# Output projection of a two-layer mixer trunk: four of eight column blocks as two seven-product pairs

## The chip, the cores and the metric

One core of a Trainium2 chip runs the whole program. The metric is device time in microseconds of one execution, the median over runs. Engines: TensorE (PE) multiplies, VectorE (DVE), ScalarE (ACT) and GpSimd (POOL) work on elements, SyncE (SP) issues the DMAs.

## The reference, cut to what matters

Two layers of width 1024 over 1024 tokens, and a final norm. The change lies in the last lines of each layer: three branch outputs are projected, gated and summed, the sum goes through one 1024 x 1024 output projection, is scaled per channel and added to the residual.

```python
def hybrid_layer(x, ...):
    ...
    proj = h @ w_in
    ...
    y = jnp.einsum('btnw,nwd->btnd', branches, w_branch)
    gates = jax.nn.sigmoid(gate_logits.reshape(B, T, N_BRANCHES, D))
    merged = jnp.sum(gates * y, axis=2)
    return x + gate * (merged @ w_out)

def reference(...):
    for l in range(DEPTH):
        x = hybrid_layer(x, ...)
    return rms_norm(x, final_g)
```

## The kernel before, in words

**Layout.** Everything is held transposed: channels on the 128 partitions, tokens along the row. The tokens form two halves `h` of 512 (HF), the 1024 channels eight blocks `d` of 128. An output tile (d, h) is one PSUM accumulator of 128 x 512; there are three of them (`acc_ps`, pool `psa`).

**Split operands.** Each fp32 operand is split into a high part `hi` (a copy rounded to fp32r, made on ScalarE) and a low part `lo` = x - hi (made on GpSimd or VectorE); function `split`. A product is three matmuls, hi x hi, hi x lo and lo x hi (`mm1`, `mm3`), so a block of 128 x 512 weights (four k-tiles of 128) takes 12 matmuls, and a column of the output projection over a token half (eight k-tiles) 24.

**Order.** Nothing is issued while the code runs. Each call is recorded as an `Op` in a `Log`; `Log.plan` then simulates the engines with costs of its own and gives every engine a fixed order, smallest key first among what is ready (the key is about the place in the program). All is issued from one line, 548, so every row of the profile reads L548, and rows are told apart by tiles. `plan` also has buffers handed out in order of first use, keeps GpSimd and VectorE instructions with several SBUF inputs apart in its own time, and may move a GpSimd `tensor_tensor` of the plain lanes to VectorE (`flex`); an instruction written for VectorE stays there. Side work (norms, splits of branch outputs, adaLN columns) runs as generators in lanes ("norm", "norm2", "ada", ...), advanced by `pump` between matmuls; `finish` forces one to its end.

**Weights.** `plan_layer` yields the items of a layer in order; `wprep` loads the next item (two 256 KB tiles `wr`, 128 x 512 each) and splits it into `wh`, `wl` (three buffers each), ahead of use (`wready`). The input projection ends with pairs of items computed as seven block products in place of eight (item "forms"; `wforms` makes the weight forms, `form` the operand forms, `prod` issues one product of 12 matmuls).

**Branches and merge.** Items ("br", n, d) for n = 0, 1, 2 and d = 0, 2, 4, 6 project branch n to blocks d and d + 1. Each tile is scaled by its gate (VectorE, PSUM input) and added into `m`, a slice of four 128 x 2048 tiles `mt` (tag r8, four buffers in all). After branch 2 each (d, h) is split into `mhi`, `mlo` (`merged[d][h]`).

**Output projection.** Part 0 takes half 0 for d = 0 to 7, part 1 half 1. In the second layer half 1 is done in two parts of 256 tokens, and the weights of columns 2 to 7, split in part 0, are kept for parts 1 and 2. Each column: load the residual tile `xres`, 24 matmuls, then on VectorE xres = acc * mod + xres, then the sum of squares (`sq_acc`: square on ScalarE, add on VectorE). In the first layer each result is stored to `xd` and, at the end of a half, `norm_task` makes the next layer's operands of that half (`hhi`, `hlo`) in lane "norm2"; the second layer starts with three items of half 0, then of half 1, whose weights (`wbig`) are loaded at the end of part 1. In the second layer `final_task` norms and stores each part.

Of the kernel before, what the change touches and what calls it, by code (L numbers as in the profile page):

```python
# [9 lines left out]
F32 = mybir.dt.float32  # L10
# [10 lines left out]
L = 2  # L21
# [49 lines left out]
def BR(n, *ds):  # L71
    return [("br", n, d) for d in ds]
# [489 lines left out]
def trunk_kernel(ctx, tc, xT, cvec, pos, vecs, consts, w_ada, w_all, pool_w, lora_w, out):  # L562
# [26 lines left out]
    def nm(s):  # L589
        uid[0] += 1  # L590
        return f"{s}_{uid[0]}"
# [384 lines left out]
    def plan_layer(l):  # L976
        yield from [("lora",)] + RW(0)
        pools = deque(PL(i) for i in range(4))
        gates = deque(GT(0, *range(8)) + GT(1, *range(8)) + GT(2, *range(8)))
        done = 0  # L980
        while done < 4 or prog.get((l, 3), 0) < 10 or pools:
            if done < 4 and prog.get((l, done), -1) >= 0:
                done += 1
                if done < 4:
                    yield from RW(done)
                if l == 0 and done == 1:
                    yield from pools.popleft()
# [12 lines left out]
        rest = list(gates) + [("wg", i) for i in range(4)]  # L1000
        yield ("forms", [(rest[i], rest[i + 1]) for i in range(0, len(rest), 2)])
        for n in range(3):
            yield from BR(n, 0, 2, 4, 6)
# [5 lines left out]
    wready = deque()  # L1009

    def wprep(big=False):
        if wready and wready[-1][0][0] == "forms":
            return
        for l, it in planner:
            if it[0] not in ("merge", "idle", "forms"):
# [7 lines left out]
        if it[0] == "out" and it[1] >= 2 and kept(l):  # L1023
            if it[2]:
                wready.append((it, keep_w[it[1]]))
                return
            if it[1] < 6:
                t = r8("wout")
            else:
                if it[1] == 6:  # L1030
                    keep_w["G"] = gtile("wG")
                t = keep_w["G"][:, 2048 * (it[1] - 6) : 2048 * (it[1] - 5)]
        elif big:
            t = r8("wbig")
        parts = []
        for j in range(2):
# [12 lines left out]
        wready.append((it, parts))  # L1049
# [901 lines left out]
    for l in range(L):  # L1951
# [245 lines left out]
            gates[key] = gs_used[key]("gs")  # L2197
            return gates[key]

        brs = deque((n, d) for n in range(3) for d in (0, 2, 4, 6))  # L2200

        def prefetch():
            for j in range(min(2, len(brs))):
                n, d0 = brs[j]
                for d in (d0, d0 + 1):
                    if (n, d, 0) not in gates:
                        if j and len(gs_free) < 7:
                            return
                        for h in range(2):
                            nc.sync.dma_start(out=gate_tile((n, d, h)), in_=gd[n, d, h])  # L2210

        unsplit = deque()
        next_o(1, 0)
        mt = [r8("mrg") for _ in range(4)]
        merged = [[None, None] for _ in range(8)]
        while wready[0][0][0] != "out":
            it, ws = wready.popleft()
            prefetch()
# [9 lines left out]
            else:  # L2228
                n, d0 = it[1], it[2]
                assert brs.popleft() == (n, d0)  # L2230
                if (n, d0) == (1, 4):
                    next_o(2, 0)
                for d, h in [(d, h) for h in range(2) for d in (d0, d0 + 1)]:
# [5 lines left out]
                    o = (d % 2) * T + h * HF  # L2239
                    m = mt[d // 2][:, o : o + HF]  # L2240
# [7 lines left out]
                    merged[d][h] = m  # L2248
# [10 lines left out]
            finish("ada", task)  # L2259
        h_next = [[], []]  # L2260
        ntask = [None, None]
        if l + 1 < L:
            parts = [(0, slice(0, HF)), (1, slice(0, HF))]
        else:
            parts = [(0, slice(0, HF)), (1, slice(0, HF // 2)), (1, slice(HF // 2, HF))]
        for part, (h, sl) in enumerate(parts):
            if sl.start == 0:
                xs = [None] * 8
                acc = t_rk("ssum")
            for i, d in enumerate(out_order(l, part)):  # L2270
                it, ws = wready.popleft()
                assert it == ("out", d, part)
                last = (i, h) == (7, 1)
# [7 lines left out]
                if sl.start == 0:  # L2281
                    xr = (mi if h == 0 else t_ri if d < 7 else t_rk)("xres")
                    src = xT if l == 0 else xd[0]
                    nc.sync.dma_start(out=xr, in_=src[d, h])
                    xs[d] = xr
                xr = xs[d][:, sl]
# [4 lines left out]
                nc.vector.scalar_tensor_tensor(  # L2291
                    xr, ps, mod[l][:, 16 + d : 17 + d], xr, op0=ALU.mult, op1=ALU.add
                )
                if l + 1 < L:
                    store(xd[0][d, h], xr)
                if d == 7:
                    sq = mo("sq")[:, sl]
                    nc.vector.tensor_tensor(sq, xr, xr, op=ALU.mult)
                    if l + 1 == L:
                        warm = sp.tile([P, 4], F32, tag="rn", name=nm("warm"))[:, 0:1]  # L2300
                        nc.scalar.activation(warm, acc[:, 0:1], AF.Sqrt)
                else:
                    sq_acc(acc[:, sl], xr, i == 0)
                if l + 1 == L:
                    nc.scalar.activation(xr, xr, AF.Copy, scale=vv(0, "final_g", d))
            if l + 1 < L:
                drain("ada")
                ntask[h] = add("norm2", norm_task(l + 1, xs, [acc, sq], h_next[h], 2500 + 2500 * h, h))
            else:
                add("norm", final_task(list(xs), [acc[:, sl], sq], h, sl))  # L2310
# [111 lines left out]
```

## Time and profile before

| | |
|---|---|
| median of 3 runs | 2262.69 us (2262.41 to 2262.93) |
| profiled execution | 2262.4 us; its span, first to last instruction, 2260.6 us |
| granted TensorE clock | 0.997 |
| PE / PEld busy | 2229.0 / 1865.3 us |
| DVE / ACT / POOL busy | 1589.5 / 931.5 / 627.0 us |
| output projection, first layer | about 1060 to 1153 us of the span |
| output projection, second layer | about 2153 to 2251 us |

Times in rows are from the start of the span. A row of a timeline is start, length, engine, line, operation, out<-in, shape, count, and in brackets the idle time of the engine before it with what ended it. A row of groups is engine, operation, tiles, shape, count, then busy time and mean length in ns, then idle time before. A matmul's recorded length (about 0.39 us for 512 columns) overlaps the next one's; the spacing of starts is what it occupies. PEld are the weight loads, which run beside the matmuls.

### The profile page before, as it was taken

To read this page: it belongs to the slowest core of one execution; us is meant where nothing else is said; L and a number is where in the kernel's file an instruction comes from. 1 tells how busy PE (TensorE), PEld (TensorE's weight loads), DVE (VectorE), ACT (ScalarE), POOL (GpSimd) and SP (SyncE) were. 2 spreads that over 40 slices of the span, in tenths; PEclk is the share of its full clock that TensorE was granted. 3 is DMA by queue.
4 is the path that set the end of the run, shared out by engine and by line. 5 is a ranking of instruction groups with operands and counts; after the bars stand their busy time and mean duration, and the time that the engine had idled before them with its cause. 6 is when DMAs were issued, how large, how long until landed. Compare 5 with 4: busy or idle time off the path is not lost.

```text
span 2260.6 us, 34881 instructions
## 1 busy us (share of the span) xinstructions
PE 2229.0 (99%) x12980; PEld 1865.3 (83%) x12980; DVE 1589.5 (70%) x2750; ACT 931.5 (41%) x1795; POOL 627.0 (28%) x564
## 2 busy tenths in 40 slices
PE   7999999999999999999999999999999999999998
PEld 6788888888888888888878888888888888888888
DVE  7996877958878765668667678587686744465854
ACT  5634434434344344323454343353443444442243
POOL 2223323323325233332122132333332500041311
PEclk9999999999999999999999999999999999999999
DMA  8222111112236664654541111111122533256442
GB/s 318 70 59 72 34 43 42 51 46 70 86 119 218 200 201 130 229 187 167 172 134 31 45 41 44 55 38 49 40 82 93 182 112 112 89 184 218 135 131 85
DMA packets 138906, 249.36 MB, mean 110 GB/s; under 512 B 15728, under 2 KB 20080, under 8 KB 138736
## 3 DMA queue, kind: packets, MB, share of 16 engines
q1 hardware_dynamic: 138736, 247.14, 34.1%
q8 instruction: 102, 1.67, 0.3%
q14 instruction: 68, 0.56, 0.1%
HBM read 187.57 MB, written 59.51 MB: 109 GB/s over the span
## 4 chain that ended last, share of the span: by engine, by line
PE 89%; DVE 7%; ACT 2%; issue 1%; DMA 1%; SPq 0%; DVEq 0%; ACTq 0%
PE acc L548 73%; PE two L548 3%; PE ch L548 2%; PE ro L548 1%; PE g L548 1%; PE av L548 1%; DVE two L548 1%; DVE tm L548 1%; DVE ksq L548 1%; PE rs L548 1%; DVE G L548 1%; PE rkv L548 1%; PE m L548 1%; PE bt L548 1%; PE lw L548 1%
## 5 line engine op out<-in xcount | busy, mean ns | idle before, releaser
L548 PE MATMUL acc<-hhi,wh 128*128 128x512 f32 x1488 | 597.1, 401 | 1.6 <-DVE vp L548 1.1
L548 PE MATMUL acc<-hhi,wl 128*128 128x512 f32 x1488 | 596.9, 401 | 0.0
L548 PE MATMUL acc<-hlo,wh 128*128 128x512 f32 x1488 | 596.3, 401 | 0.0
L548 POOL TENSOR_TENSOR wl<-wr,wh 128x512 fp32r<-128x512 f32 x171 | 228.4, 1335 | 585.8 <-ACT wh L548 440.5
L548 PEld LDWEIGHTS acc<-hhi,wh 128*128 128x128 f32 x1488 | 280.5, 189 | 50.8 <-DVE vp L548 1.5
L548 PEld LDWEIGHTS acc<-hhi,wl 128*128 128x128 f32 x1488 | 280.6, 189 | 48.7
L548 PEld LDWEIGHTS acc<-hlo,wh 128*128 128x128 f32 x1488 | 280.6, 189 | 47.3
L548 ACT CAST wh<-wr 128x512 fp32r<-128x512 f32 x242 | 149.3, 617 | 268.3 <-PE acc L548 215.5
L548 PE MATMUL acc<-T,wh 128*128 128x512 f32 x576 | 177.6, 389 | 0.0
L548 PEld LDWEIGHTS acc<-T,wh 128*128 128x128 f32 x576 | 108.1, 188 | 22.4
L548 DVE SCALAR_TENSOR_TENSOR S<-ch,pc,SP 64x64 f32<-64x64 f32 x224 | 63.3, 283 | 87.1 <-PE ch L548 84.3
L548 PE MATMUL acc<-T,wl 128*128 128x512 f32 x288 | 112.1, 389 | 0.0
L548 DVE TENSOR_TENSOR wl<-wsum,wh 128x512 fp32r<-128x512 f32 x63 | 45.3, 719 | 78.7 <-ACT wh L548 78.4
L548 ACT CAST wh<-wsum 128x512 fp32r<-128x512 f32 x96 | 59.5, 620 | 96.6 <-PE acc L548 92.9
L548 ACT COPY Z<-ch 64x128 f32<-64x128 f32 x128 | 33.0, 258 | 132.6 <-PE ch L548 132.0
L548 POOL TENSOR_TENSOR oz<-ol,oz 128x512 fp32r<-128x512 f32 x10 | 14.0, 1401 | 264.8 <-DVE wl L548 179.7
L548 DVE TENSOR_TENSOR tm<-MT,two 64x30 f32<-64x30 f32 (+14 forms) x240 | 76.3, 318 | 11.4 <-ACT two L548 4.6
L548 DVE TENSOR_TENSOR two<-two,tm 64x30 f32<-64x30 f32 (+14 forms) x240 | 78.9, 329 | 7.1
L548 PE MATMUL acc<-oy,wh 128*128 128x512 f32 x256 | 80.1, 394 | 0.0
L548 PE MATMUL acc<-oG,wh 128*128 128x512 f32 x256 | 79.0, 390 | 0.0
L548 PE MATMUL acc<-oz,wh 128*128 128x512 f32 x256 | 78.9, 389 | 0.0
L548 DVE TENSOR_TENSOR wl<-wraw,wh 128x512 fp32r<-128x512 f32 x48 | 33.7, 703 | 63.5 <-ACT wh L548 63.5
(332 smaller groups left out, 4863.5 us busy)
## 6 DMA issues: line engine op xcount, KB each, us to landing
wr<-in_w_all SPq DMA_DIRECT2D x268, 256.0 KB, 2.7
wraw<-in_w_all SPq DMA_DIRECT2D x96, 256.0 KB, 2.7
gd<-gsg SPq DMA_DIRECT2D x96, 256.0 KB, 2.0
gs<-gd SPq DMA_DIRECT2D x96, 256.0 KB, 3.8
wada<-in_w_ada SPq DMA_DIRECT2D x80, 256.0 KB, 2.9
ol<-od SPq DMA_DIRECT2D x48, 256.0 KB, 3.5
traw<-hd SPq DMA_DIRECT2D x32, 256.0 KB, 3.0
x<-in_xT SPq DMA_DIRECT2D x16, 256.0 KB, 5.2
```

Of the source, the lines that this page charges most:

```text
L548: o.inst = f(*a, **k)
```

## The change

Columns d = 0 to 3 leave the column-by-column scheme. Part 0 keeps columns 4 to 7 of half 0. Then a new item ("outs",) computes the pairs (0, 1) and (2, 3) for both halves, each as seven block products: with A the two columns' weights in four blocks (column x k-half) and B the merged operand in four blocks (k-half x token half), products of sums and differences of blocks replace the eighth. Then part 1 (and 2) does columns 4 to 7 of half 1.

- `out_forms(f)`, four tasks in lane "norm2", makes the operand forms: in place on the raw merged tiles (`raw_m`, whose layout in `mt` is changed to one tile per d-half and token half), three subtractions per k for f = 0, one for f = 1, none for 2 and 3; each form is then split, high half on ScalarE, low half on VectorE. Task 0 is added at the last item of branch 2, tasks 1 to 3 at columns 0, 1, 3 of part 0 (`TAT`). Low halves of forms 1 to 3 take an r8 buffer each, high halves of forms 2 and 3 the big tile G.
- `out_pairs` makes the weight forms: four loads, four combinations on VectorE and seven splits with the low half on VectorE (`osplit_w`) per pair.
- Products accumulate in three accumulators; `add_out` adds an accumulator into the residual tile more than once (seven adds in the first pair, six in the second, against four for the same tiles before).
- `wprep`'s low halves of branch 2 and of part 0 are made on VectorE. Branch 2 takes its items in the order 0, 4, 2, 6. In the second layer columns 5 to 7 are kept from part 1 for part 2, column 4 is loaded again.

```diff
+TAT = (0, 1, 3)
+DORDER = ((0, 2, 4, 6), (0, 2, 4, 6), (0, 4, 2, 6))
...
     def out_order(l, part):
-        return (2, 3, 0, 4, 5, 1, 6, 7) if kept(l) and part else range(8)
+        return (5, 6, 4, 7) if part == 2 else (4, 5, 6, 7)
...
         for part in range(2 + (l + 1 == L)):
+            if part == 1:
+                yield ("outs",)
             yield from [("out", d, part) for d in out_order(l, part)]
...
-            split(raw, hi, lo)
+            split(raw, hi, lo, nc.vector if it[0] == "out" and it[2] == 0 or it[:2] == ("br", 2) else nc.gpsimd)
...
+        def out_forms(f):
+            if f == 2:
+                out_G.append(gtile("oT"))
+            if f:
+                oL = r8("oL")
+                los = [oL[:, k * HF : (k + 1) * HF] for k in range(4)]
+            else:
+                los = [t_ri("oL") for _ in range(4)]
...
+            for k in range(4):
+                while any(type(merged[q][h]) is not tuple for q in (k, k + 4) for h in range(2)):
+                    yield 2000
+                b11, b12, b21, b22 = raw_m[k][0], raw_m[k][1], raw_m[k + 4][0], raw_m[k + 4][1]
+                if f == 0:
+                    sub_(b11, b12, b11)
+                    sub_(b12, b22, b12)
+                    sub_(b22, b22, b11)
+                elif f == 1:
+                    sub_(b21, b21, b22)
+                x = (b11, b22, b12, b21)[f]
...
+                nc.scalar.copy(hi, x)
+                nc.vector.tensor_tensor(lo, x, hi.bitcast(F32), op=ALU.subtract)
...
+                for d in (0, 2):
+                    xr = [[residual(d + i, h_) for h_ in range(2)] for i in range(2)]
+                    ca = acc_ps()
+                    prod(ca, lows[0], True)
+                    cd, cb = acc_ps(), acc_ps()
+                    nc.scalar.copy(cb, ca)
+                    if d == 0:
+                        prod(cd, highs[1], True)
+                        add_out(d, xr[0][1], cd)
+                        finish("norm2", otasks[0])
+                        cd = acc_ps()
+                        prod(cd, OT[0], True)
+                        add_out(d + 1, xr[1][1], cd)
+                        add_out(d, xr[0][1], cd)
+                        finish("norm2", otasks[1])
+                        prod(cb, OT[1], False)
+                        add_out(d, xr[0][1], cb)
+                        out_done(d, 1, full, True, False)
+                        prod(ca, highs[0], False)
+                        add_out(d, xr[0][0], ca)
+                        out_done(d, 0, full, False, False)
+                        finish("norm2", otasks[2])
+                    else:
+                        prod(cd, OT[0], True)
+                        add_out(d + 1, xr[1][1], cd)
+                        prod(cb, OT[1], False)
+                        add_out(d, xr[0][1], cb)
+                        prod(ca, highs[0], False)
+                        add_out(d, xr[0][0], ca)
+                        out_done(d, 0, full, False, False)
+                    prod(cb, OT[2], False)
+                    add_out(d + 1, xr[1][1], cb)
+                    out_done(d + 1, 1, full, False, False)
+                    if d:
+                        prod(cd, highs[1], False)
+                        add_out(d, xr[0][1], cd)
+                        out_done(d, 1, full, False, False)
+                    finish("norm2", otasks[3])
+                    prod(cb, OT[3], False)
+                    add_out(d + 1, xr[1][0], cb)
+                    out_done(d + 1, 0, full, False, d == 2)
+                half_done(0, full)
...
+                if part == 0 and i == 3:
+                    source = out_pairs()
+                    ready_w.extend(next(source) for _ in range(2))
+                if part == 0 and i in TAT:
+                    otasks.append(add("norm2", out_forms(len(otasks))))
```

`out_done` is what followed the add before (store, square, final scale); `half_done(0)` starts the norm of half 0 and now stands after the pairs; `residual` loads a residual tile once per (d, h).

More of the change, by code (lines that the diff above doesn't have):

```diff
@@ L2261, in trunk_kernel, with residual @@
         ntask = [None, None]
+        xs = [[None] * 8, [None] * 8]
+        late = deque()
+        acc = [None, None]
+        sqs = [None, None]
+        def residual(d, h):
+            if acc[h] is None:
+                acc[h] = t_vp("ssum")
+            if xs[h][d] is None:
+                if h and d == 2:
+                    late.extend([r8("xres")] * 4)
+                if h and 2 <= d < 6:
+                    xr = late.popleft()[:, (d - 2) * HF : (d - 1) * HF]
+                else:
+                    xr = (mi if h == 0 else t_ri if d < 7 else t_rk)("xres")
+                nc.sync.dma_start(out=xr, in_=(xT if l == 0 else xd[0])[d, h])
+                xs[h][d] = xr
+            return xs[h][d]
@@ new lines, in add_out, with out_done @@
+        def add_out(d, xr, ps):
+            nc.vector.scalar_tensor_tensor(xr, ps, mod[l][:, 16 + d : 17 + d], xr, op0=ALU.mult, op1=ALU.add)
+        def out_done(d, h, sl, first, last):
+            xr = xs[h][d][:, sl]
+            if l + 1 < L:
+                store(xd[0][d, h], xr)
+            if last:
+                sqs[h] = mo("sq")[:, sl]
+                nc.vector.tensor_tensor(sqs[h], xr, xr, op=ALU.mult)
+                if l + 1 == L:
+                    warm = sp.tile([P, 4], F32, tag="rn", name=nm("warm"))[:, 0:1]
+                    nc.scalar.activation(warm, acc[h][:, 0:1], AF.Sqrt)
+            else:
+                sq_acc(acc[h][:, sl], xr, first)
+            if l + 1 == L:
+                nc.scalar.activation(xr, xr, AF.Copy, scale=vv(0, "final_g", d))
@@ new lines, in half_done, with osplit_w @@
+        def half_done(h, sl):
+            if l + 1 < L:
+                drain("ada")
+                ntask[h] = add("norm2", norm_task(l + 1, xs[h], [acc[h], sqs[h]], h_next[h], 2500 + 2500 * h, h))
+            else:
+                add("norm", final_task(list(xs[h]), [acc[h][:, sl], sqs[h]], h, sl))
+        def osplit_w(x):
+            hi = wp.tile([P, HF], F32R, tag="wh", name=nm("wh"), bufs=3)
+            lo = wp.tile([P, HF], F32R, tag="wl", name=nm("wl"), bufs=3)
+            split(x, hi, lo, nc.vector)
+            return hi, lo
@@ new lines, in out_pairs, with loads, comb, forms @@
+        def out_pairs():
+            def loads(d):
+                r = []
+                for it, j in ((("out", d), 0), (("out", d + 1), 0), (("out", d + 1), 1), (("out", d), 1)):
+                    r.append(t_rk("wraw"))
+                    nc.sync.dma_start(out=r[-1], in_=w_all[l, ITEMS.index(it), j])
+                return r
+            def comb(x, y, op):
+                t = t_cs("wsum")
+                nc.vector.tensor_tensor(t, x, y, op=op)
+                return t
+            def forms():
+                for d in (0, 2):
+                    a11, a21, a22, a12 = loads(d)
+                    yield osplit_w(a11)
+                    s1 = comb(a21, a22, ALU.add)
+                    if d:
+                        yield osplit_w(s1)
+                    s2 = comb(s1, a11, ALU.subtract)
+                    if d:
+                        yield osplit_w(s2)
+                    else:
+                        yield osplit_w(comb(a12, s2, ALU.subtract))
+                    if d == 0:
+                        yield osplit_w(s1)
+                        yield osplit_w(s2)
+                    yield osplit_w(a12)
+                    yield osplit_w(comb(a11, a21, ALU.subtract))
+                    if d:
+                        yield osplit_w(comb(a12, s2, ALU.subtract))
+                    yield osplit_w(a22)
+            return forms()
@@ L2280, in trunk_kernel @@
                             wprep()
[L2281 to L2286, printed above, removed]
+                xr = residual(d, h)[:, sl]
                 ps = acc_ps()[:, 0 : xr.free_size()]
@@ L2290, in trunk_kernel @@
                     mm3(ps, ws[j], rhs, j == 0, j == 1)
[L2291 to L2310, printed above, removed]
+                add_out(d, xr, ps)
+                out_done(d, h, sl, part == 0 and i == 0, h == 1 and i == 3)
+            if h == 1:
+                half_done(1, sl)
         drain("norm", "st") if l + 1 == L else None
```

54 lines of the change are left out of this document (38 added, 16 removed).

## The prediction

> **What bounds the kernel now.** I read the page's first and fourth parts first, then the chain of waits in order of time for the long stretches without a break, then a table of busy times over the stages around the output projection, and last VectorE's and GpSimd's timelines there.
>
> ```profile
> span 2260.6 us, 34881 instructions
> PE 2229.0 (99%) x12980; PEld 1865.3 (83%) x12980; DVE 1589.5 (70%) x2750; ACT 931.5 (41%) x1795; POOL 627.0 (28%) x564
> PE 89%; DVE 7%; ACT 2%; issue 1%; DMA 1%; SPq 0%; DVEq 0%; ACTq 0%
> ...
> 1786.80 411.03 PE acc L548 x1807
> 2205.94 19.55 PE acc L548 x163
> 2229.82 20.03 PE acc L548 x167
> ```
>
> TensorE is the bound: 99% busy, 89% of the chain. A busy share says little by itself, since matmuls overlap in the records, so the price of a matmul is its spacing in an unbroken piece of the chain. 1807 matmuls in 411.03 us are 0.2275 us each; that piece runs from the second layer's seven-product pairs of the input projection through the branch products into the output projection, so such pairs already stream without a gap. In the last stretch the matmuls have 256 columns: 163 in 19.55 and 167 in 20.03 us, 0.1199 us each. Two of them do one wide matmul's work in 0.2398 us.
>
> The stages, from the last branch's product (n = 2) of the first layer through its two output halves to the start of the second layer, and the second layer's last branch product and output halves. Columns after the window: its length, then busy time and count by engine, clock, DMA share, GB/s.
>
> ```profile
> 1016.50:1060.20 43.70, 43.70 (x192) 35.78 (x191) 37.61 (x47) 13.31 (x22) 11.31 (x9) 1.00 0.51 171
> 1060.20:1104.00 43.80, 43.80 (x199) 36.38 (x198) 23.42 (x34) 15.43 (x25) 1.39 (x2) 1.00 0.47 148
> 1104.00:1148.00 44.00, 44.00 (x203) 36.69 (x202) 31.51 (x43) 22.59 (x37) 14.81 (x12) 1.00 0.59 193
> 1148.00:1180.00 32.00, 30.20 (x144) 24.67 (x143) 24.77 (x38) 20.03 (x36) 10.04 (x12) 1.00 0.45 143
> ...
> 2109.00:2153.00 44.00, 44.00 (x192) 35.82 (x191) 38.52 (x47) 12.85 (x22) 13.23 (x10) 1.00 0.43 136
> 2166.00:2210.00 44.00, 44.00 (x237) 38.09 (x236) 19.89 (x31) 18.11 (x31) 5.16 (x4) 1.00 0.35 106
> ```
>
> In every stage that the change touches TensorE has no idle time except 1.8 us at the start of the second layer. So fewer matmuls shorten the run, unless what they need comes later. VectorE is next: 86% in the branch stage (37.61 of 43.70), 53% in the first output half.
>
> **The matmuls removed.** A column of 128 outputs over half of the tokens takes 8 x 3 = 24 matmuls. First layer now: 8 columns x 2 halves x 24 = 384 wide ones, 87.4 us. After: part 0 has 4 x 24 = 96, the two pairs 2 x 7 x 12 = 168, part 1 another 96, together 360, 81.9 us: 5.5 us less. Second layer now: 192 wide and 384 narrow ones, 192 x 0.2275 + 384 x 0.1199 = 89.7 us. After: 96 + 168 wide and 192 narrow, 60.1 + 23.0 = 83.1 us: 6.6 us less, since the pairs also run at full width what ran in halves. Together **12.1 us**, with 24 + 120 = 144 matmuls fewer.
>
> **VectorE's load, the cover of everything else.** What a VectorE instruction costs there:
>
> ```profile
> 1011.23 0.69 DVE L548 SCALAR_TENSOR_TENSOR gs<-gs,acc 128x512 f32<-128x512 f32 x1 [1.36 <-PE acc L548]
> 1011.84 0.69 DVE L548 TENSOR_TENSOR oG<-ol,oG 128x512 fp32r<-128x512 f32 x1
> 1012.44 1.79 DVE L548 TENSOR_TENSOR mrg<-mrg,gs 128x512 f32<-128x512 f32 x1
> ...
> 1058.44 1.29 POOL L548 TENSOR_TENSOR wl<-wr,wh 128x512 fp32r<-128x512 f32 x1 [6.02 <-ACT wh L548]
> 1058.53 1.75 DVE L548 TENSOR_TENSOR mlo<-mrg,mhi 128x512 fp32r<-128x512 f32 x1
> 1060.20 0.68 DVE L548 TENSOR_TENSOR mrg<-mrg,gs 128x512 f32<-128x512 f32 x1
> ```
>
> Independent instructions start 0.60 us apart though each lasts 0.69. One that starts beside a GpSimd low half lasts 1.75 and the next starts 1.67 us later, so each such meeting costs VectorE 1.67 - 0.60 = 1.07 us. Moving a low half of a branch weight from GpSimd to VectorE therefore costs 0.60 and may return 1.07; with 8 per layer the branch stage gets no fuller.
>
> From the start of the last branch product to the end of the pairs, per layer, VectorE then has: branch stage 3 x 16 for the merging and its low halves, 8 weight low halves and about 2 others, 58; part 0, 8 weight low halves, 4 residual adds and 3 sums of squares, 15; the operand forms, 16 subtractions and 16 low halves, 32; the pairs, 8 weight combinations, 14 low halves, 7 + 6 residual adds and 7 squares, 42. Sum 147. At an estimated 0.64 (between 0.60 and 0.69) that is 94 us; TensorE takes 43.7 + 21.8 + 38.2 = 103.7. It fits at 91%. The tightest place is the first pair's seventh product, which needs the fourth form: from the end of the branch stage to it TensorE takes 21.8 + 6 x 2.73 = 38.2 us, and VectorE has part 0's 15, the forms' 32, 4 combinations, 7 low halves, 6 adds and 2 squares, 66 x 0.64 = 42.2, less the 8 of the first form that it can make in the branch stage's last 11 us (5.1): 37.1. Price taken: 0. If the cover goes, VectorE sets the pace; that is the first rival.
>
> Trainium skill, VectorE: DVE Perf Modes, section The DRAIN you can't avoid: the next instruction waits until the pipe of the one before is empty, though its next section lets one that is not held start earlier. By the first half VectorE would need 147 x 0.69 = 101 us, and the margin would be 2 us; the starts 0.60 apart show the second half here. Trainium skill, SBUF — State Buffer, section Who interferes with whom: an instruction with two SBUF inputs and a GpSimd one that reads SBUF lock each other out for a whole instruction. The 1.75 agrees; by it the moved low halves give VectorE 8 x (1.07 - 0.60) = 3.8 us per branch stage, and without it they would take 4.8.
>
> **Other added work.** ScalarE: 16 high halves, 2 copies between PSUM tiles; 16 x 0.62 + 2 x 0.58 = 11 us on some 21 that it would do in those 60 us (15.43 of 43.8): hidden; if not, it delays VectorE's low half by one copy. DMAs: a pair loads four 256 KB tiles where two columns took eight over both halves; SP issues fewer in all (wr 22 fewer, wraw 16 more); cost 0, and if a load is late the weights are two products of 2.7 us ahead of it. The operand forms take the 2048-wide buffers in turn (each form's low halves wait until the form before has freed one); late forms show as waits of TensorE in the first pair, counted next.
>
> ```profile
> L548 DVE SCALAR_TENSOR_TENSOR xres<-acc,mod,xres 128x512 f32<-128x512 f32 x24 | 18.0, 750 | 34.0 <-PE acc L548 33.7
> L548 ACT CAST wh<-wsum 128x512 fp32r<-128x512 f32 x96 | 59.5, 620 | 96.6 <-PE acc L548 92.9
> L548 ACT COPY acc<-acc 128x512 f32<-128x512 f32 x24 | 13.9, 577 | 3.2 <-PE acc L548 3.2
> L548 POOL TENSOR_TENSOR wl<-wr,wh 128x512 fp32r<-128x512 f32 x171 | 228.4, 1335 | 585.8 <-ACT wh L548 440.5
> L548 PE MATMUL acc<-hhi,wl 128*128 128x512 f32 x1488 | 596.9, 401 | 0.0
> ```
>
> **New waits in the first pair of each layer.** There are three accumulators. The second product's must be added into the residual before the third product may take it, and the sixth's before the seventh adds onto it. The bare turn: the last matmul runs out its 0.40 past the 0.23 spacing, 0.17, then the add, 0.75, and two hand-overs, about 1.0 us in all; 1.7 where another instruction is in front of the add. Two places in two layers: 0 (the list order lets TensorE go on with another product whose weights are there) to 6.8 us. For the sixth the next pair's first product is free to run; for the second the fourth product needs the second form and a weight that is only just split. I take 1.0 at the second product and 0 at the sixth: **2.0 us**.
>
> **The start of the second layer.** The norm of the first half now begins after the pairs and has 4 columns (21.8 us) of cover, not 8 (43.7).
>
> ```profile
> 1105.11 0.75 DVE L548 SCALAR_TENSOR_TENSOR xres<-acc,mod,xres 128x512 f32<-128x512 f32 x1 [2.51 <-PE acc L548]
> 1110.78 4.87 DVE L548 TENSOR_TENSOR xres<-xres,rbc 128x512 f32<-128x512 f32 x8 [0.91 <-PE rbc L548]
> 1129.39 2.29 DVE L548 TENSOR_TENSOR hlo<-xres,hhi 128x512 fp32r<-128x512 f32 x2
> ...
> 1113.66 1.30 POOL L548 TENSOR_TENSOR wl<-wr,wh 128x512 fp32r<-128x512 f32 x1 [4.45 <-ACT wh L548]
> 1131.96 1.48 POOL L548 TENSOR_TENSOR wl<-wr,wh 128x512 fp32r<-128x512 f32 x1 [1.42 <-ACT wh L548]
> ...
> PE acc L548 <- DVE r L548: 1.8, 1, 1.8
> ```
>
> It took from 1105.1 to 1131.7, 26.6 us. The new cover is 21.8 plus the 21 matmuls of the first item that come before its last k-tile, 4.8: also 26.6. So 0 if the order holds; if all of 4.8 shows, and the second half's norm is pushed by as much, 9.6. Below, the 1.8 us wait that stands there could go. VectorE had 8 GpSimd low halves beside that norm (the first and the last of them shown), and part 1 still has 8. I take **1.0**, near the lower end, because three items of 24 matmuls are there to be interleaved.
>
> **The second layer's end.** Columns 5 to 7 are split again in part 1, at 2.9 us per column; GpSimd alone makes two low halves in 2.7, and VectorE can help. Their big buffer comes free with the pairs' last product, 5.8 us before column 6 needs it. Price 0; at worst one column late, 2. The chain after the last matmul is as before. New places in the order also shift what follows in the second layer (how many gates are projected singly, 48 against 42 matmuls, 1.4 us each): 0, +-1.5.
>
> **Sum.** The profiled execution took 2262.4 (span 2260.6): 2262.4 - 12.1 + 2.0 + 1.0 = 2253.3. The median of the runs shown is 2262.69, 0.3 more, so **2253.6**, a span of 2251.5.
>
> **Rivals.** (1) VectorE becomes the bound, and it is slower. In the branch stage of before its instructions averaged 0.80 (37.61 over 47). If they still do, 147 x 0.80 = 117.6 us against 103.7: 13.9 per layer, 2262.7 - 12.1 + 27.8 = 2278. It decides from 0.747 on, where (103.7 + 6.05) / 147 eats the gain. For it: the in-place forms are chains of dependent instructions, and nothing of it can move to GpSimd any more. Against: the 0.80 holds the GpSimd meetings, which the change removes; without them the next stage has 0.69 busy per instruction (23.42 over 34). (2) The norm at the start of the second layer loses its cover: all 9.6 show and the 2.0 stay: 2262.7 - 12.1 + 11.6 = 2262.2, no change. For it: cover and need are equal to 0.1 us. Against: only 25 of 32 us of VectorE are taken there. (3) All waits are filled: 2262.7 - 12.1 - 0.5 = 2250. For it: the pairs of the input projection run so.
>
> **How the numbers follow.** Forecast 0.56, all filled 0.20, norm uncovered 0.13, VectorE bound 0.11. Measurement tells about 0.2% (4.5 us) from no change, so faster is below 2258.2. The forecast and rival 3 are faster in full, rival 2 is same but for 0.02, and rival 1 is slower in 0.09 and same in 0.02: **faster 0.78, same 0.13, slower 0.09**. The range reaches from rival 3 with a drift of -1.5, 2249, to most of rival 2, 2261; the likeliest case's own is 2251 to 2257.
>
> **What would show it.** Right: 12836 matmuls; pieces of the chain through the pairs at 0.2275 per matmul; ScalarE's accumulator copies x28, not x24; GpSimd nearly idle from the last branch product to the end of the pairs, and VectorE's 1.75 us instructions gone there; stage lengths 43.7, 21.8, 38.2 to 40, 21.8 in the first layer. Wrong: TensorE idle in the first pair behind the forms' low halves with VectorE over 95% (rival 1), or more than 3 us of idle TensorE behind the norm's or the evictions' instructions after the first layer (rival 2). A TensorE count well off 12836 would say that the order of the second layer changed elsewhere.

## The result, and the profile after

| | before | after |
|---|---|---|
| median | 2262.73 us (2262.41 to 2266.53) | **2251.2 us** (2250.74 to 2255.68) |
| profiled execution / its span | 2262.4 / 2260.6 | 2251.25 / 2249.4 |
| matmuls | 12980 | 12836 |

Both were run in 5 rounds. The ratio is 0.9949, 95% interval [0.9935, 0.9962]: the changed kernel is faster by 11.5 us (8.6 to 14.7). The prediction was 2253.6 in 2249 to 2261. Ratios compare the executions in the faster state; of all that are shown here, one of extra_half's eleven, at 8274 us, was in the slower.

The page of the kernel after, first part, and the longest unbroken piece of its chain of waits (start, length, what, number of matmuls):

```profile
span 2249.4 us, 34694 instructions
PE 2214.6 (98%) x12836; PEld 1847.6 (82%) x12836; DVE 1637.2 (73%) x2865; ACT 953.6 (42%) x1829; POOL 595.3 (26%) x538
...
1782.41 424.31 PE acc L550 x1867
```

TensorE has 144 matmuls and 14.4 us of busy time less, VectorE 115 instructions more, GpSimd 26 fewer. The spacing is what it was, 424.31 / 1867 = 0.2273 us, so the time came out of the count and not out of faster matmuls.

Busy times by stage of the kernel after (window, length, then TensorE, its weight loads, VectorE, ScalarE, GpSimd with counts, clock, DMA share, GB/s): the last branch, part 0, the two pairs, part 1 and the start of the second layer; then part 0, the pairs and the rest in the second layer.

```profile
1016.00:1059.70 43.70, 43.70 (x192) 35.78 (x191) 41.36 (x68) 16.26 (x28) 0.28 (x1) 1.00 0.47 139
1059.60:1081.40 21.80, 21.80 (x98) 18.05 (x97) 21.54 (x36) 13.31 (x24) 0.00 (x0) 1.00 0.46 159
1081.40:1119.60 38.20, 38.20 (x174) 31.74 (x173) 27.66 (x44) 14.63 (x24) 0.00 (x0) 1.00 0.46 146
1119.60:1141.60 22.00, 22.00 (x107) 18.50 (x106) 18.14 (x27) 13.76 (x23) 8.75 (x8) 1.00 0.65 214
1141.60:1184.60 43.00, 40.27 (x185) 32.01 (x184) 36.28 (x50) 24.98 (x45) 18.48 (x17) 1.00 0.38 127
...
2151.70:2173.50 21.80, 21.80 (x98) 18.05 (x97) 21.55 (x36) 15.31 (x27) 0.00 (x0) 1.00 0.41 131
2173.50:2211.70 38.20, 38.20 (x174) 31.74 (x173) 28.79 (x46) 21.94 (x36) 0.00 (x0) 1.00 0.30 86
2211.70:2239.90 28.20, 27.64 (x229) 27.21 (x227) 17.19 (x37) 11.42 (x26) 4.60 (x4) 1.00 0.46 156
```

Part 0 takes 21.8 us and the pairs 38.2, in both layers, and TensorE is busy for all of it. VectorE is busy for 21.54 of 21.80 in part 0: it is full there, and nothing waits for it yet. From the last branch product to the end of the pairs GpSimd is busy for 0.28 us in all.

TensorE's waits, first from 1010 to 1200 us and then from 2100 us to the end (what waited, for whom, total, times, longest):

```profile
PE acc L550 <- DVE r L550: 1.5, 1, 1.5
PE lw L550 <- DVE xres L550: 0.7, 1, 0.7
PE ssps L550 <- DVE ssum L550: 0.4, 1, 0.4
PE acc L550 <- POOL hlo L550: 0.2, 1, 0.2
...
PE ssps L550 <- DVE sq L550: 1.0, 1, 1.0
PE rbc L550 <- DVE rn L550: 0.6, 1, 0.6
PE ssps L550 <- DVE ssum L550: 0.6, 1, 0.6
```

The first four stand at the start of the second layer and make 2.8 us, against 1.8 before. Of the last three the first two are the chain behind the last matmul, which was there before too; the third is new.

To see where the time came from, every kernel below is cut at the first matmul of each layer's output projection and at the last matmul of its columns:

| kernel | first layer's projection begins | to the second layer's | from there to the last matmul | tail |
|---|---|---|---|---|
| before | 1060.4 | 1096.0 | 94.0 | 10.2 |
| after | 1059.6 | 1092.1 | 88.0 | 9.7 |
| pairs_first | 1063.2 | 1092.1 | 93.9 | 9.8 |
| pairs_second | 1060.0 | 1095.9 | 87.2 | 10.6 |
| lows_gpsimd | 1059.8 | 1093.3 | 89.2 | 10.3 |
| lows_only | 1060.5 | 1096.0 | 93.9 | 10.3 |
| three_first | 1060.7 | 1092.1 | 88.9 | 10.0 |
| three_second | 1060.5 | 1092.1 | 89.9 | 12.8 |
| extra_vector | 1059.7 | 1104.9 | 100.4 | 9.8 |
| extra_half | 1060.1 | 1095.3 | 91.6 | 10.2 |
| extra_late | 1061.5 | 1093.2 | 88.7 | 9.8 |
| pair_order | 1058.9 | 1092.0 | 87.5 | 9.8 |

The first column scatters between 1058.9 and 1063.2, so single profiles are compared by the columns behind it. Between before and after, the first layer brings 3.9 us, the second 6.0 and the tail 0.5; 0.8 of the 11.2 us between the spans arose ahead of the first cut.

### The profile page after: what moved, and what is told of

Its sections match the earlier page's. It is cut to its first block, busy times and chain, and to the rows that moved or that the text cites. A ratio compares the mean times of both kernels' runs of the same rounds, so it can differ in the third digit from the quotient of the medians.

```text
span 2249.4 us, 34694 instructions
## 1 busy us (share of the span) xinstructions
PE 2214.6 (98%) x12836; PEld 1847.6 (82%) x12836; DVE 1637.2 (73%) x2865; ACT 953.6 (42%) x1829; POOL 595.3 (26%) x538
## 5 line engine op out<-in xcount | busy, mean ns | idle before, releaser
L550 POOL TENSOR_TENSOR wl<-wr,wh 128x512 fp32r<-128x512 f32 x143 | 189.8, 1327 | 474.9 <-ACT wh L550 343.2
L550 ACT CAST wh<-wr 128x512 fp32r<-128x512 f32 x226 | 139.5, 617 | 251.1 <-PE acc L550 191.3
L550 ACT CAST wh<-wsum 128x512 fp32r<-128x512 f32 x112 | 69.5, 621 | 121.1 <-PE acc L550 117.3
L550 DVE TENSOR_TENSOR wl<-wsum,wh 128x512 fp32r<-128x512 f32 x79 | 56.2, 712 | 79.0 <-ACT wh L550 78.7
L550 DVE TENSOR_TENSOR wl<-wraw,wh 128x512 fp32r<-128x512 f32 x60 | 42.0, 699 | 63.2 <-ACT wh L550 63.2
L550 ACT CAST wh<-wraw 128x512 fp32r<-128x512 f32 x84 | 52.0, 619 | 70.8 <-PE acc L550 50.1
```

The lines of the kernel that those rows point to most:

```text
L550: o.inst = f(*a, **k)
```

## The experiments

Each ran in 5 rounds beside the kernel before, and "faster" below is against that. They are kernels of the change unless said otherwise. The diffs are cut, and show what an edit does where the files do it by shared parameters. The kernel after was not run again beside them: where its interval overlaps that of another kernel of the change (lows_gpsimd, three_first, extra_late, pair_order), the times alone don't tell the two apart, and the profile's columns have to. The branch order (0, 4, 2, 6) and the columns of `TAT` were not varied by themselves.

**One layer alone: pairs_first, pairs_second.** The number of pairs becomes a parameter of the layer; a layer with 0 is as before.

```diff
+NP = (2, 0)        # pairs in the first and second layer; (0, 2) in the other kernel
...
-            if part == 1:
+            if part == 1 and NP[l]:
                 yield ("outs",)
```

> Pairs in the first layer alone; the second layer's output projection is as before. Theory A, the gain is the matmuls removed, layer by layer: 24 wide matmuls of 0.2275 us less, 5.5 us, less about 1.0 us of added waits at the start of the second layer (2.8 us of TensorE waits after the change there, 1.8 before): 2262.7 - 4.5 = 2258.2 us. Theory B, the start of the second layer eats the first layer's gain and all of it comes from the second layer: 2262 us.

> Pairs in the second layer alone; the first layer's output projection is as before. Theory A: 120 matmuls less, 24 wide ones' worth and 192 narrow ones in place of 96 wide, 6.6 us, less 0.6 us for the wait on the last sum of squares that the trace after the change shows: 2262.7 - 6.0 = 2256.7 us. Theory B, all of the 11.5 us come from the second layer: 2251 us. The two gains should add up to the whole change's 11.5 us by A to about 1 us.

Measured: pairs_first 2258.74 (ratio 0.9987 [0.9978, 0.9996], 2.9 us faster), pairs_second 2255.69 (0.9970 [0.9960, 0.9979], 6.8 us faster). The sum, 9.7, lies in the interval of the whole change. In the table each layer's column is that of the kernel after where it has pairs (1092.1; 87.2 to 88.0) and that of before where it has none: the two layers add up and don't disturb each other, as theory A has it in both. The second layer's larger part is what the count of matmuls says (its 192 wide and 384 narrow ones become 264 and 192), while the first layer gives some of its 5.5 back.

**The low halves on VectorE: lows_gpsimd, lows_only.** The first takes this part out of the change, the second makes it alone.

```diff
-            split(raw, hi, lo, nc.vector if it[0] == "out" and it[2] == 0 or it[:2] == ("br", 2) else nc.gpsimd)
+            split(raw, hi, lo, nc.gpsimd)     # lows_gpsimd; lows_only: NP = (0, 0) and this line left as it is
```

> The whole change, but the low halves of the branch 2 weights and of part 0's weights are left to GpSimd as before (28 of the 32 in two layers go there). Theory A, VectorE is loaded almost to the full up to the pairs (41.4 of 43.7 us and 21.5 of 21.8 us busy) and each meeting with a GpSimd low half costs it 1.07 us where its own low half costs 0.60: the forms end about 14 x 0.47 = 6.6 us later per layer, of which 1 to 4 us per layer show as waits of TensorE in the first pair: 2253 to 2259 us. Theory B, VectorE has room enough for either: 2251 us, no change against the whole change.

> The kernel before, with those low halves alone (branch 2 and part 0) made on VectorE; no pairs, 12980 matmuls. Theory A: TensorE is not waiting for them, so 2262.7 us, within 0.2%. Theory B, the low halves are a good part of the gain: 2257 us or less.

Measured: lows_gpsimd 2255.07 (0.9968 [0.9955, 0.9980]), lows_only 2262.37 against 2262.13 (1.0003 [0.9994, 1.0012]). Alone the move brings nothing. Beside the pairs the medians differ by 3.9 us, of which the columns show 1.2 in each layer and 0.6 in the tail; the intervals of the two kernels overlap, so the 1.2 per layer is the surer part, and the tail's 0.6 is no more than tails differ between the other kernels (9.7 to 10.6, three_second aside). Busy times of lows_gpsimd in the first layer (branch stage, part 0, pairs), TensorE's one wait there, and one of VectorE's instructions of part 0 in its timeline (start, length, operation, what ended the idle time):

```profile
1016.00:1059.80 43.80, 43.80 (x193) 35.88 (x192) 40.20 (x56) 15.83 (x27) 11.50 (x9) 1.00 0.44 138
1059.80:1081.60 21.80, 21.80 (x98) 18.06 (x97) 19.32 (x25) 11.94 (x22) 8.66 (x6) 1.00 0.49 158
1081.60:1120.90 39.30, 38.73 (x175) 31.75 (x174) 32.87 (x52) 16.27 (x27) 0.00 (x0) 1.00 0.46 144
...
PE acc L552 <- DVE oL L552: 0.6, 1, 0.6
...
1063.36 1.77 DVE L552 TENSOR_TENSOR mrg<-mrg,gs 128x512 f32<-128x512 f32 x1
```

VectorE gets 56 instructions done in the branch stage and 25 in part 0, in place of 68 and 36: beside GpSimd's low halves single ones last 1.77 us again, not 0.69. Of these 12 and 11 fewer, 14 are the low halves that GpSimd makes here (15 on GpSimd in the two stages against 1); the other 9 VectorE did not get to. It has to do them in the pairs (52 in place of 44), and TensorE waits for a low half of an operand form, 0.6 us per layer, which is less than the 1 to 4 of theory A. So the move takes no work off VectorE, it adds 14 instructions; but without the long meetings VectorE does them and 9 more in the same time, at the place where the forms are due.

**The order in the first pair: pair_order.** The first pair gets the order of products of the second, with one add into the residual fewer.

```diff
-                    if d == 0:
-                        prod(cd, highs[1], True)
-                        add_out(d, xr[0][1], cd)
-                        ...
+                    finish("norm2", otasks[0])
+                    prod(cd, OT[0], True)
+                    add_out(d + 1, xr[1][1], cd)
+                    finish("norm2", otasks[1])
+                    prod(cb, OT[1], False)
+                    ...
```

> The first pair of each layer takes its products in the second pair's order: the first operand form is used at the second product, one product (2.7 us) earlier, there is no second use of an accumulator right behind its add, and one residual add less. Theory A, the forms are ready that early (in the trace after the change VectorE is through all four 5.8 us after the pairs begin): 2251 us, no change. Theory B, the forms come too late for it and TensorE waits 1 to 3 us per layer: 2253 to 2257 us.

Measured: 2251.19 (0.9952 [0.9940, 0.9965]), the time of the kernel after. Its columns are the same within 0.5 us, and TensorE has no wait in either pair. The 0.5 is at the second layer's end: the wait of 0.6 us for ssum, last in the list of the kernel after, is missing here. The first pair's own order, which takes products that need no form ahead of the forms, shows no gain here: the written order is not what TensorE follows anyway, since the recorded list is put in order anew.

**More pairs: three_first, three_second.** Columns 0 to 5 as three pairs in one layer, two pairs in the other; part 0 then has columns 6 and 7, with one form's task added at the first and two at the second.

```diff
+NP = (3, 2)        # (2, 3) in the other kernel
...
-                for d in (0, 2):
+                for d in range(0, 2 * NP[l], 2):
```

> Three pairs in the first layer, two in the second: 12 wide matmuls less, 2.7 us. The cover of the first half's norm at the start of the second layer falls from 21.8 to 10.9 us, while that norm needs 26.6. Theory A, the three first items of the second layer are interleaved and hide it: 2248.5 us, with the waits there still near 3 us. Theory B, the cover counts once it falls below the need: 5 to 10 us more of TensorE waits there, 2254 to 2259 us.

> Three pairs (columns 0 to 5) in the second layer, two in the first. Removed again: part 0 has 48 wide matmuls, the pairs 252, parts 1 and 2 96 narrow ones: 68.3 + 11.5 = 79.8 us against 83.1, 3.3 us less. Theory A, VectorE still keeps ahead of the pairs: 2251.2 - 3.3 = 2248 us. Theory B, with 10.9 us of cover in part 0 in place of 21.8 the operand forms come too late (VectorE had 0.3 us idle in part 0 already), TensorE waits 3 to 8 us in the first pair: 2251 to 2256 us.

Measured: three_first 2253.34 (0.9958 [0.9944, 0.9971]), three_second 2256.49 (0.9972 [0.9961, 0.9984]). They have 12 and 60 matmuls fewer than the kernel after, and their medians are 2 and 5 us above its own; for three_first that is within the intervals, but the 2.7 us are not there either. Neither theory had the reason. In the first, the column of the layer stays at 1092.1: the 2.7 us saved are gone again at the start of the second layer, though the waits there are 2.3 us and not more than the 2.8 of the kernel after. Its busy times there, and TensorE's timeline:

```profile
1144.00:1148.00 4.00, 2.73 (x17) 2.52 (x17) 4.00 (x6) 3.97 (x8) 1.42 (x2) 0.85 0.97 303
1148.00:1152.00 4.00, 4.00 (x11) 3.23 (x12) 3.08 (x6) 0.69 (x2) 3.85 (x3) 0.50 0.91 312
1152.00:1156.00 4.00, 4.00 (x19) 3.37 (x19) 0.43 (x1) 1.34 (x3) 2.49 (x4) 0.79 0.25 74
...
1144.70 0.49 PE L552 MATMUL acc<-hhi,wbig 128*128 128x512 f32 x1 [0.75 <-ACT wbig L552]
1145.04 1.02 PE L552 MATMUL ssps<-fixed,ssum 128*128 128x1 f32 x8
1146.63 1.72 PE L552 MATMUL ssps<-fixed,sq 128*128 128x1 f32 x8 [0.57 <-DVE sq L552]
1148.21 0.77 PE L552 MATMUL acc<-hlo,wbig 128*128 128x512 f32 x1
```

The two waits shown are small, 0.75 and 0.57. But from 1143.95 to 1148.21 TensorE ran one wide matmul and 16 of one column, and then the granted clock is 0.50 for 4 us and 0.79 for 4 more: 4 x 0.50 + 4 x 0.21 = 2.8 us of matmul time lost, the whole gain. The busy column hides it, since a slow matmul is a busy one. The 0.9 more in its second layer goes with the wait for ssum, 1.5 us in place of 0.6.

three_second has no wait in its pairs, so the forms don't come too late (theory B), but the same fall of the clock in its last stage (window 2226 to 2232, its waits ahead of that, and those at the end):

```profile
2223.00:2226.00 3.00, 1.71 (x12) 1.42 (x12) 2.90 (x4) 2.26 (x5) 1.40 (x1) 0.88 0.00 0
2226.00:2229.00 3.00, 3.00 (x14) 3.00 (x15) 0.60 (x2) 0.62 (x1) 0.24 (x1) 0.50 0.37 93
2229.00:2232.00 3.00, 3.00 (x16) 3.00 (x16) 0.51 (x1) 0.00 (x0) 1.03 (x1) 0.50 0.00 0
...
PE acc L552 <- ACT wG L552: 0.7, 1, 0.7
PE acc L552 <- DVE wG L552: 0.6, 1, 0.6
PE ssps L552 <- DVE sq L552: 3.4, 2, 3.1
```

Six us at half the clock are 3 us lost, and the kept weights wG come late by 1.3. With only two columns in the last part the final norm has less cover: TensorE waits 3.1 us for the last squares, 1.0 in the kernel after, which is most of the longer tail (12.8 against 9.7).

**VectorE's margin: extra_vector, extra_half, extra_late.** Low halves are computed again into the same place: those of the operand forms three times and twice, and in the last one those of the pairs' weight forms twice.

```diff
+                for _ in range(3):            # extra_half: range(2)
                     nc.vector.tensor_tensor(lo, x, hi.bitcast(F32), op=ALU.subtract)     # in out_forms
...
             split(x, hi, lo, nc.vector)                                                  # in osplit_w
+            nc.vector.tensor_tensor(lo, x, hi.bitcast(F32), op=ALU.subtract)             # extra_late
```

> The whole change with every low half of the operand forms made three times over (same result): 32 more VectorE instructions per layer, 19.2 us at 0.60. VectorE's work from the last branch product to the end of the pairs goes from 90.6 to 109.8 us per layer, TensorE's is 103.7. Theory A, VectorE has only that slack: 6.1 us per layer by the sum and 7 to 10 if the forms' end (1087.2, moved to 1106) is what the pairs wait for: 2263 to 2271 us, so the change's gain is gone, as rival 1 of the prediction put its turning point. Theory B, the order hides it: 2251 us.

> The changed kernel with each low half of an operand form made twice in place of once: 16 more VectorE instructions per layer, 9.6 us, a total of about 100 us on VectorE in 103.7 us of TensorE's. Theory A (the sum decides: VectorE is the bound only if its instructions of the whole stretch don't fit): 2251 to 2253. Theory B (the deadline decides: the forms are ready 5.8 us after the pairs begin, and 9.6 us later TensorE stands still for some 2 us per layer, after which its clock is lowered for a while, so that each us of standing costs two): 2256 to 2264.

> The changed kernel with each low half of a weight form of the pairs made twice in place of once: 14 more VectorE instructions per layer, 8.4 us, nearly the number of the run before, but in the pairs, behind most of the operand forms. Theory A (the sum decides): the same as the run before, 2251 to 2253. Theory B (the deadline of the operand forms decides, and only the few of these that come ahead of it push it): 2251 to 2254, and at least 3 us faster than the run with doubled operand forms.

Measured, with the instructions added per layer:

| kernel | added per layer | time | ratio to before | added to each layer's column |
|---|---|---|---|---|
| after | | 2251.2 | 0.9949 [0.9935, 0.9962] | |
| extra_late | 14 (8.4 us) in the pairs | 2253.94 | 0.9960 [0.9948, 0.9973] | 1.1, 0.7 |
| extra_half | 16 (9.6 us) in the forms | 2259.77 | 0.9985 [0.9976, 0.9994] | 3.2, 3.6 |
| extra_vector | 32 (19.2 us) in the forms | 2278.27 | 1.0069 [1.0057, 1.0082] | 12.8, 12.4 |

Nearly the same number of instructions costs 2.7 us in one place and 8.6 in the other (1.8 and 6.8 in the columns), though VectorE's totals are 99 and 100 us in 103.7. So the sum over the whole stretch does not decide alone: it matters what else VectorE has to finish behind the added work, and when that is due. In the kernel after the last low half of a form is written at about 1087.2, 5.8 us after the pairs begin (VectorE's timeline, the last forms' low halves and the first gap behind them):

```profile
1085.98 1.29 DVE L550 TENSOR_TENSOR oL<-mrg,oT 128x512 fp32r<-128x512 f32 x2
1087.19 0.74 DVE L550 SCALAR_TENSOR_TENSOR xres<-acc,mod,xres 128x512 f32<-128x512 f32 x1
1087.85 0.68 DVE L550 TENSOR_TENSOR wl<-wraw,wh 128x512 fp32r<-128x512 f32 x1
1091.09 1.41 DVE L550 SCALAR_TENSOR_TENSOR xres<-acc,mod,xres 128x512 f32<-128x512 f32 x2 [2.55 <-PE acc L550]
```

In extra_late it is written at 1093.4, in extra_half at 1109.2. There TensorE never waits for a form: its gaps follow VectorE's and ScalarE's weight forms and an eviction (the add of an accumulator into the residual), which stand behind doubled low halves in VectorE's order (VectorE's last low halves of the forms, then TensorE's timeline):

```profile
1105.33 3.82 DVE L552 TENSOR_TENSOR oL<-mrg,oT 128x512 fp32r<-128x512 f32 x6
...
1102.38 0.49 PE L552 MATMUL acc<-oT,wh 128*128 128x512 f32 x1 [0.57 <-ACT wh L552]
1103.06 0.50 PE L552 MATMUL acc<-oT,wh 128*128 128x512 f32 x1 [0.20 <-DVE xres L552]
1103.40 0.40 PE L552 MATMUL acc<-oL,wh 128*128 128x512 f32 x1
1104.27 0.51 PE L552 MATMUL acc<-oT,wl 128*128 128x512 f32 x1 [0.47 <-DVE wl L552]
```

Here theory B gave the time, but not for its reason: the clock stays at 1.00, and no gap is longer than 0.6. The gaps make 1.3 us of the 3.2 in this layer; the rest stands in the starts around them, which lie further apart than 0.2273. extra_vector, slower than both its theories, has a long gap, which does end with a form's low half, and the clock follows (busy times around it, then TensorE's timeline):

```profile
1094.00:1098.90 4.90, 1.02 (x5) 0.52 (x3) 4.88 (x9) 1.25 (x2) 0.00 (x0) 0.89 0.45 153
1098.90:1104.50 5.60, 5.29 (x11) 3.11 (x12) 5.59 (x10) 1.25 (x2) 0.00 (x0) 0.50 0.15 55
1104.50:1108.00 3.50, 3.50 (x16) 2.80 (x15) 3.41 (x7) 0.93 (x2) 0.00 (x0) 0.97 0.00 0
...
1098.93 0.79 PE L552 MATMUL acc<-oL,wh 128*128 128x512 f32 x1 [3.91 <-DVE oL L552]
1103.21 0.63 PE L552 MATMUL acc<-mlo,wh 128*128 128x512 f32 x1
1103.64 0.63 PE L552 MATMUL acc<-oL,wh 128*128 128x512 f32 x1
```

After 3.91 us without a matmul these start 0.43 us apart, at a clock of 0.50. The next stretch of waits brings it down again, and over 1100 to 1119.7 it is 0.79 on the mean. In the first layer the waits make 6.4 us, and 9.2 us of matmuls at half the clock some 4.6, most of the 12.8 that the column grew. By the sum alone 19.2 us of added work against 13.1 us of cover would have cost 6.1.

## Why the prediction was right, and where it was off

**The bound and the removed matmuls: right.** 12836 matmuls and a spacing of 0.2273 us; 12.1 us were to go, 5.5 and 6.6 by layer, and the columns of the layers gave 3.9 and 6.0: the difference is what follows.

**The waits in the first pair, 2.0 us: not there.** This is the term that was mis-sized. It measured 0: the pairs' window holds 38.20 us of busy TensorE in 38.20. The end of the second product in TensorE's timeline:

```profile
1086.58 0.39 PE L550 MATMUL acc<-mhi,wl 128*128 128x512 f32 x1
1086.80 0.39 PE L550 MATMUL acc<-oT,wh 128*128 128x512 f32 x1
```

The next product starts 0.22 us behind it, while the add that frees the accumulator begins only at 1087.19 (the xres row above): so TensorE took a product that needs no freed accumulator, and its form was ready. Among the seventh product's it runs matmuls of the next pair (mhi rows from 1097.7). pair_order shows that it doesn't hang on the written order. The lower end of my own range, "the list order lets TensorE go on with another product", was the case; I had taken the fourth product's weights and form to be only just late.

**The start of the second layer, +1.0: right.** The waits there are 2.8 us against 1.8. The wait that I thought could go (for r) became 1.5 and stayed, 1.1 came with the norm's residual and sums, and 0.2 with a low half. The first layer's column gained 3.9, which is 5.5 less 1.0 and 0.6. For this last 0.6 the rows give an estimate: the matmul ahead of a wait is recorded for 0.39 us, 0.16 more than its spacing, and the start after the first one behind a wait comes 0.34 later, 0.11 more, so that a wait takes about 0.27 beside its idle time. Three waits more than before make 0.8. No run tests this alone.

**The second layer's end, 0: off by 0.6.** VectorE's final multiplications wait for their output tile to be stored, and TensorE for a sum of squares behind them (VectorE's timeline of the kernel after, then TensorE's):

```profile
2222.59 2.51 DVE L550 TENSOR_TENSOR fin<-xres,rbc 128x512 f32<-128x512 f32 x4 [1.90 <-DMA out_t<-fin]
...
2227.09 0.58 PE L550 MATMUL ssps<-fixed,ssum 128*128 128x1 f32 x4 [0.56 <-DVE ssum L550]
```

It accounts for the second layer's column: 6.6 less 0.6 is the 6.0 measured, and pair_order, which lacks this wait, has 0.5 less.

**VectorE's cover: right in size, but it is not a margin.** Counted from 1015.9 to 1119.6 it has 148 instructions (147 forecast) and 90.6 us, 0.61 each (0.64 taken). Part 0 is full at 99%. The tightest place that I worked out, the seventh product with the fourth form, was not as tight: in the 38.2 us up to it, 1059.6 to 1097.8, VectorE is busy for 35.4, where I had 37.1, and the form is done 10.6 us ahead. Where rival 1 would decide was put wrong. By the prediction's sum the gain is gone when VectorE needs 103.7 + 6.05 = 109.8 us per layer, 19.2 more than the 90.6 measured. That is just what extra_vector adds, and it is not even with the kernel before but 16 us slower. Between extra_half (2.9 us faster than before, with 9.6 added) and extra_vector a straight line crosses zero at about 11 us: by this estimate the margin is little more than half of what the sum says, for work at that place. The sum lets work be done late that a product already waits for, and it has no term for the clock.

**The low halves: right.** The meetings of 1.75 us are gone, GpSimd shows 0.28 us in the branch stage and 0 in part 0 and the pairs, and lows_gpsimd brings the meetings back. The rule of the Trainium skill, SBUF — State Buffer, section Who interferes with whom, which the prediction weighed, agrees: 1.77 beside GpSimd, 0.69 without it.

**ScalarE and the buffers, 0: right.** 28 accumulator copies, and no wait of TensorE on a load or a copy in these stages.

In all, profile against profile: forecast 2253.3, measured 2251.25. The waits in the pairs take off 2.0, the tail 0.5 and the stretch ahead of the change 0.8; the second layer's end adds 0.6 and the rest of the first layer 0.6: -2.1 of the -2.05. The 0.8 ahead of the change is chance, and so may the tail's 0.5 be, so the 2253.6 came this near partly by luck: the terms of the changed stages by themselves were off by -2.0 and +1.2. The result lies between the forecast and the rival with all waits filled, 2250.

## What to carry to other kernels

Where TensorE streams without a gap, matmuls removed are worth their spacing, and the question is only what their operands cost elsewhere. Give the engine that makes these operands a deadline and not only a sum: a few per cent of margin in the total did not help extra_half, whose added work stood ahead of what TensorE needed next. Moving an engine's instructions can bring nothing in itself (lows_only) and yet pay when it ends the meetings of two engines at the place where time is short.

## What the runs showed of the hardware that was not expected

**A pause of TensorE can cost more than its length.** After 3.91 us without a matmul the granted clock was 0.50, and matmuls started 0.43 us apart in place of 0.2275. The clock fell already in the pause, and stayed there for 6.8 us (1097.85 to 1104.68 in extra_vector). The same came in a stretch of 4.3 us with one wide matmul and 16 of one column (three_first, half clock from 1146.8 to 1153.7), and in one of 3.3 us with three narrow ones and eight of one column (three_second, 2225.3 to 2232.1). One-column matmuls did not keep the clock up there, although they count as busy. It did not come with the waits of 1.8 us before, of 1.5 after, or of 0.57 in extra_half. But the longest pause alone does not decide: extra_vector's second fall, 3.4 us long, came behind a pause of 1.28 us only. Busy times of the 3.4 us ahead of that fall and of the fall, then of the 3.4 us that hold the 1.8 us wait of the kernel before:

```profile
1108.10:1111.50 3.40, 1.89 (x7) 0.97 (x6) 3.40 (x7) 1.33 (x3) 0.00 (x0) 1.00 0.20 77
1111.50:1114.90 3.40, 3.40 (x9) 2.66 (x8) 3.40 (x6) 0.17 (x1) 0.00 (x0) 0.50 0.52 154
...
1173.60:1177.00 3.40, 2.08 (x10) 1.39 (x8) 3.40 (x6) 2.89 (x5) 0.00 (x0) 1.00 0.49 185
```

How little work it takes for a fall, these runs leave open.

The Trainium skill, TensorE: Matmul & The Clock Gate, Part 1, says that the clock falls to half after an idle window of about 3.4 us and comes back after about as long a busy one, with the window's phase free. The lengths of the falls agree, 3.4 us and twice that; but the 3.4 us ahead of the second fall were not idle, since TensorE is busy for 1.89 of them. I had no term for the clock, since no wait of the forecast was longer than 2 us, but rival 1 would have needed one.

**The same program scatters ahead of the change.** The first layer's projection began between 1058.9 and 1063.2 us in twelve profiles, though what goes ahead of it is nearly the same program. A gain of 3 us is therefore read from the stage and from many rounds, not from one span.
